# Two-layer encoder trunk on one core: all projections by seven products of quarters, output sums kept in DRAM, one buffer layout

## The chip, the core and the metric

The kernel runs on one core of a Trainium2 chip. Its engines work side by side: TensorE multiplies (PE in the profile, with PEld for its weight loads), VectorE (DVE) and ScalarE (ACT) work on elements, GpSimd (POOL) does a few small operations and issues some transfers, and SyncE (SP) issues the other transfers. The metric is the device time of one execution in microseconds; lower is better.

## The reference

The input is x of 512 tokens by 2048 features in float32. Two layers follow, each of the form x = layer_norm(ALPHA * x + mixer(x)).

```python
def attention_mixer(h, w_in, q_gain, k_gain, w_out, cos, sin):
    proj = h @ w_in
    q, k, v, g = jnp.split(proj, [A_WIDTH, A_WIDTH + A_KV_WIDTH, A_WIDTH + 2 * A_KV_WIDTH], axis=-1)
    ...
    q = apply_rope(rms_norm(q, q_gain), cos, sin) * (A_HEAD_DIM ** -0.5)
    k = apply_rope(rms_norm(k, k_gain), cos, sin)
    ...
        p = jax.nn.softmax(s, axis=-1).astype(v.dtype)
    ...
    return (o * jax.nn.silu(g)) @ w_out

def retention_mixer(h, w_in, decay_exp, w_out, cos, sin):
    proj = h @ w_in
    ...
    fwd = chunk_retention(q, k, v, log_g[0], strict=False)
    bwd = jnp.flip(chunk_retention(jnp.flip(q, 1), jnp.flip(k, 1), jnp.flip(v, 1), log_g[1], strict=True), 1)
    o = head_group_norm(fwd + bwd).reshape(B, S, R_V_WIDTH)
    return (o * jax.nn.silu(g)) @ w_out
```

Layer 1 is attention with 16 query heads of 128 and 4 key and value heads: w_in is 2048 x 5120, w_out 2048 x 2048. Layer 2 is retention with 8 heads (256 for q and k, 512 for v and the gate): w_in is 2048 x 12288, w_out 4096 x 2048. Nearly all the arithmetic is in these four projections.

## The kernel before, in words

**Arithmetic.** Every float32 operand is split into a high and a low part in a rounded format (`split`, L116 to L119: ScalarE casts the high part, VectorE subtracts it for the low part). A product is three matmuls, hi*hi, hi*lo and lo*hi (`mm3`, L261 to L265). A weight chunk is 128 x 1024 (512 KB): loaded by SyncE (`raw_load`), split by ScalarE and VectorE (L118 and L119, or L244 and L246 in layer 1 and the output projections), and used by TensorE in 12 or 24 matmuls. `next_chunk` keeps two chunks made ahead of the one in use (AHEAD = 2), and three pairs of chunk buffers (wp) hold them.

**Order of work.** TensorE's instructions stand in the order of the program text. Work that can wait is a generator (`Stream`), and `pump(us)` runs so many microseconds of it between the steps of a latency-bound part. So attention and retention steps are laced with projection matmuls.

**Layer 1** goes by four groups. For each: q by 512-wide matmuls (`n_form`), the rotary and norm work (`q_group`), attention (`att_group`: `scores`, four transposes and a split in `turn`, and `values`, which takes two heads together as 256 moving columns), laced with the gate projection (`t_form`, 512 wide), the next group's k and v (256 wide) and the last group's output projection (`out_proj`). The sums of the output projections stay in SBUF in y, added by VectorE (`accumulate`, L325 and L327).

**Between the layers** `out_proj_last` goes token block by token block, `norm_1` normalises, `turn_1` transposes into four quarters (token half by feature half), and the pools of layer 1 are closed before those of layer 2 open.

**Layer 2's input projection** is already done by quarters: the product of a 2x2 block matrix by seven block products instead of eight. `group(g)` goes through the seven products p; the activations' combinations are made once (`form`), the weights' combinations chunk by chunk on VectorE (`block_sum`, the adds at L212), with the names x, y and z for the three chains of PSUM banks (`CHAIN`). `evacuate` combines the banks, `deliver` rotates and transposes q and k and stores q, k, v and gates in DRAM (qkD, vD, gD).

**Retention** loads these per head, makes scores (`s_unit`, four per head), values (`o_unit`, four), norms and gates them (L880 to L884) and transposes (`o_close`). Each head's steps are laced with the output projection of the head before. At the change of pools after head 0, `residual` (L962 to L970) reads the normalised x back from DRAM and applies gain and bias. The last output projection goes token block by token block with `norm_2` and the stores of the result behind it.

## Time and profile before

| | |
|---|---|
| median of 3 timed runs | 2268.21 us (2267.46 to 2268.89) |
| the profiled execution's own time | 2264.06 us |
| its span | 2262.3 us |
| PE busy | 2188.5 us (97%) in 10448 matmuls |
| PEld / DVE / ACT / POOL busy | 81% / 70% / 42% / 9% |
| moved by DMA | 300.66 MB, mean 133 GB/s |

How to read it: matmuls are pipelined, so "busy" overlaps and the mean time of one matmul (390 ns) is not its price; the price is the distance between the starts of two in a row. A wait row reads "engine, what waited, <- what it waited for: us in total, times, longest". A group row reads "line, engine, operation, out<-in, shape xcount | busy us, mean ns | idle before". A window row reads "start:end length, busy us (count) for each engine, granted TensorE clock, share of the 16 DMA engines in use, GB/s".

### The profile page before, as it was taken

Reading aid. Unit: us, or ns where it says so; the run is one execution under the profiler, and the core shown is the slowest. Engines: PE = TensorE matmul, PEld = TensorE weight load, DVE = VectorE, ACT = ScalarE, POOL = GpSimd, SP = SyncE. Lnnn points to the kernel's source line nnn. Section 1 sums busy time; section 2 is a strip of 40 time slices with the busy share of each in tenths; the row PEclk is TensorE's granted clock in tenths of the full one; section 3 lists DMA queues with packets and bytes.
Section 4 is the critical chain, followed back from the end, with each engine's and each line's share of the span. In section 5 each row is a group of like instructions: output and inputs, shape, how many; then the busy total and the mean of one; then the engine's idle time right before and its main releaser. Section 6 shows DMA issues by size and latency. Waiting matters only on the chain.

```text
span 2262.3 us, 27514 instructions
## 1 busy us (share of the span) xinstructions
PE 2188.5 (97%) x10448; PEld 1830.5 (81%) x10448; DVE 1590.7 (70%) x2419; ACT 956.8 (42%) x1399; POOL 204.0 (9%) x247
## 2 busy tenths in 40 slices
PE   9999999999999979999999999999997699999997
PEld 8898888889888768888888888888886488888886
DVE  5565654655567897867787788778786766666667
ACT  4353243244245744444444444444464333333331
POOL 1201100200200000000000000000003400000004
PEclk9999999999999989999999999999999799999999
DMA  7312312322323364554465445545555433333332
GB/s 279 94 47 84 94 65 84 91 68 67 104 73 94 121 226 161 189 179 142 143 204 159 131 160 187 168 136 180 186 178 175 140 112 124 128 112 126 106 122 75
DMA packets 83557, 300.66 MB, mean 133 GB/s; under 512 B 10337, under 2 KB 11617, under 8 KB 81121
## 3 DMA queue, kind: packets, MB, share of 16 engines
q1 hardware_dynamic: 73440, 263.25, 36.0%
q0 software_dynamic: 9984, 35.66, 4.5%
q8 instruction: 82, 1.34, 0.2%
q14 instruction: 51, 0.41, 0.1%
HBM read 265.31 MB, written 33.55 MB: 132 GB/s over the span
## 4 chain that ended last, share of the span: by engine, by line
PE 91%; DVE 4%; POOL 2%; DMA 1%; issue 1%; ACT 1%; SPq 0%; POOLq 0%; DVEq 0%; ACTq 0%
PE acc L263 26%; PE acc L265 26%; PE acc L264 26%; PE tr L396 3%; PE o L263 2%; PE o L265 2%; PE o L264 2%; PE s L263 1%; PE s L264 1%; PE s L265 1%; POOL y L970 1%; DMA ln_bias<-in_ln_bias_dram 1%; DVE wlo L246 1%; DVE f L119 0%; DVE q_x L446 0%
## 5 line engine op out<-in xcount | busy, mean ns | idle before, releaser
L118 ACT CAST whi<-raw 128x1024 fp32r<-128x1024 f32 (+1 forms) x340 | 356.2, 1048 | 434.2 <-PE acc L265 393.2
L263 PE MATMUL acc<-whi,f 128*128 128x512 f32 x1344 | 526.1, 391 | 12.5 <-ACT whi L118 12.1
L264 PE MATMUL acc<-wlo,f 128*128 128x512 f32 x1344 | 523.9, 390 | 0.8 <-DVE wlo L119 0.7
L265 PE MATMUL acc<-whi,f 128*128 128x512 f32 x1344 | 523.7, 390 | 0.0
L119 DVE TENSOR_TENSOR wlo<-raw,whi 128x1024 fp32r<-128x1024 f32 (+1 forms) x340 | 409.5, 1212 | 154.0 <-ACT whi L118 149.8
L246 DVE TENSOR_TENSOR wlo<-raw,whi 128x512 fp32r<-128x512 f32 x324 | 215.2, 695 | 213.1 <-ACT whi L244 212.8
L244 ACT CAST whi<-raw 128x1024 fp32r<-128x1024 f32 x162 | 170.2, 1051 | 374.9 <-PE acc L265 192.2
L263 PEld LDWEIGHTS acc<-whi,f 128*128 128x128 f32 x1344 | 252.7, 188 | 65.1 <-ACT whi L118 12.5
L264 PEld LDWEIGHTS acc<-wlo,f 128*128 128x128 f32 x1344 | 252.8, 188 | 53.4 <-DVE wlo L119 1.9
L265 PEld LDWEIGHTS acc<-whi,f 128*128 128x128 f32 x1344 | 252.7, 188 | 52.6
L212 DVE TENSOR_TENSOR raw<-raw,raw 128x1024 f32<-128x1024 f32 x192 | 231.9, 1221 | 36.6 <-DMA raw<-in_wr_in_dram 35.5
L263 PE MATMUL acc<-whi,xT 128*128 128x256 f32 (+1 forms) x512 | 175.1, 342 | 4.9 <-ACT xT L118 4.9
L263 PE MATMUL acc<-whi,og 128*128 128x512 f32 x448 | 175.8, 392 | 0.0
L265 PE MATMUL acc<-whi,og 128*128 128x512 f32 x448 | 174.6, 390 | 0.0
L264 PE MATMUL acc<-wlo,og 128*128 128x512 f32 x448 | 174.6, 390 | 0.0
L265 PE MATMUL acc<-whi,xT 128*128 128x256 f32 (+1 forms) x512 | 173.6, 339 | 0.6 <-DVE xT L119 0.6
L264 PE MATMUL acc<-wlo,xT 128*128 128x256 f32 (+1 forms) x512 | 173.2, 338 | 0.0
L327 DVE TENSOR_TENSOR y<-acc,y 128x512 f32<-128x512 f32 x160 | 107.6, 686 | 26.7 <-PE acc L265 26.1
L263 PEld LDWEIGHTS acc<-whi,xT 128*128 128x128 f32 x512 | 98.3, 192 | 16.9 <-ACT xT L118 4.9
L265 PEld LDWEIGHTS acc<-whi,xT 128*128 128x128 f32 x512 | 98.2, 192 | 11.1 <-DVE xT L119 1.0
L264 PEld LDWEIGHTS acc<-wlo,xT 128*128 128x128 f32 x512 | 98.3, 192 | 10.1
L263 PE MATMUL acc<-xT,whi 128*128 128x512 f32 x256 | 102.6, 401 | 0.0
(184 smaller groups left out, 3355.8 us busy)
## 6 DMA issues: line engine op xcount, KB each, us to landing
raw<-in_wr_in_dram SPq DMA_DIRECT2D x248, 512.0 KB, 4.3
raw<-in_wr_o_dram SPq DMA_DIRECT2D x64, 512.0 KB, 3.6
raw<-in_wa_q_dram SPq DMA_DIRECT2D x32, 512.0 KB, 3.5
raw<-in_wa_g_dram SPq DMA_DIRECT2D x32, 512.0 KB, 3.5
raw<-in_wa_o_dram SPq DMA_DIRECT2D x32, 512.0 KB, 3.5
qkD<-qkT POOLq DMA_DIRECT2D x32, 256.0 KB, 5.4
vD<-t POOLq DMA_DIRECT2D x32, 256.0 KB, 5.0
raw<-qkD SPq DMA_DIRECT2D x16, 512.0 KB, 3.8
```

Source lines behind the costliest of these rows:

```text
L118: nc.scalar.copy(hi, src)
L119: nc.vector.tensor_sub(lo, src, hi.bitcast(F32))
L212: nc.vector.tensor_add(x, x, y)
L244: nc.scalar.copy(hi, raw[:, k])
L246: nc.vector.tensor_sub(lo[:, j], raw[:, k.start + j], hi[:, j].bitcast(F32))
L263: nc.tensor.matmul(ps, sh, mh, start=start, stop=False, skip_group_check=go_on)
L264: nc.tensor.matmul(ps, sh, ml, start=False, stop=False, skip_group_check=go_on)
L265: nc.tensor.matmul(ps, sl, mh, start=False, stop=stop, skip_group_check=go_on)
L327: nc.vector.tensor_add(yc, ps, yc)
L396: nc.tensor.transpose(out=b[:, tcols(i)], in_=src[:, tcols(i)], identity=ident)
L970: nc.gpsimd.tensor_add(y[:, t, cs], y[:, t, cs], gb[1])
```

## The change

All four projections now go by seven products of quarters, with one class `Block` for the weights, one class `Operand` for the activations and one generator `products`.

- Layer 1's input projection is five blocks of 1024 columns (k and v of all groups, then q and gate of each group), stored in DRAM (kD, vD, qD, gD); attention then runs as a second stage in two parts of two groups. The first is laced with the last input block, the second with the output projection of the first two groups.
- The output projections take two groups, or two heads, at a time: 1024 features in, two blocks of 1024 columns out, 14 chunks each. Their products are copied out of PSUM by ScalarE and added to a sum in DRAM (yD1, yD2) by GpSimd transfers that accumulate (`add_out`, `onto`). Only the last pair of each layer is added in SBUF (`Final`).
- The sums of weight quarters are in part made by accumulating transfers into the loaded chunk; a VectorE add is left in p = 6, and in p = 4 of the "lean" blocks (the third and later of each input projection).
- Attention values are made with tokens in the rows, one head at a time: 128 moving columns, and the division by the softmax sum is folded into the gate.
- The first two input blocks of each layer run as products (1, 2), (1, 2) and then (5, 6, 3, 7, 4) each.
- Retention runs two heads per pump stream; the residual of layer 2 is built during four input blocks, through DRAM.
- One layout: xp with 32 tiles of 128 x 1024, 9 raw chunks, 13 temporaries, 8 PSUM banks under one tag. No pool is closed.
- Rotary multiplications of layer 1 that GpSimd did are on VectorE. In `turn_1` gain and bias of the transposed x go half to ScalarE and half to VectorE.

```diff
-    ph = Pools(hp=24, tmp=6, rp=3, yp=1)
+    xp = ctx.enter_context(tc.tile_pool(name="xp", bufs=32))
+    rp = ctx.enter_context(tc.tile_pool(name="rp", bufs=9))
+    tmp = ctx.enter_context(tc.tile_pool(name="tmp", bufs=13))
...
+    def onto(x, src):
+        nc.gpsimd.dma_start(out=x, in_=src, accum_op=ALU.add)
...
+        def fetch(self, p, c):
+            if p == 1:
+                g["v" if self.lean else 1, c] = raw_load(q(11))
+            elif p == 2:
+                g[2, c] = raw_load(q(21))
+            elif p == 5 and not self.lean:
+                g["v", c] = raw_load(q(11))
+                onto(g["v", c], q(12))
+            elif p == 6:
+                g[3, c] = raw_load(q(22))
+            elif p == 7 and not self.lean:
+                g[7, c] = raw_load(q(12))
+                onto(g[7, c], q(22))
...
+        def make(self, p, c):
+            if p == 6:
+                nc.vector.tensor_add(v, v, g[3, c])
+            if p == 4 and self.lean:
+                nc.vector.tensor_add(v, v, g[2, c])
...
+        def follow(self, p, c):
+            if self.lean and p == 1:
+                onto(g["v", c], q(12))
+            elif self.lean and p == 3:
+                onto(g[3, c], q(12))
+            elif not self.lean and p == 6:
+                onto(g["v", c], q(21))
...
+    def add_out(yD):
+        def evacuate(blk, p):
+            nb, r, sign = ADDS[p]
+            for t in range(2):
+                o = temp("yo")
...
+                    nc.scalar.copy(o, blk.bk[CHAIN[p]][t])
...
+                onto(yD[:, r + t, blk.c0 + nb * 512:blk.c0 + nb * 512 + 512], o)
...
+        def products(self, b0, b1, op):
+            for seq in ((1, 5, 6, 3, 2), (7, 4)):
+                for b in (b0, b1):
+                    yield from products(b, op, seq, self.evacuate)
...
-                mm3(ob[:, :2 * P], (v[0][:, tcols(kb)], v[1][:, tcols(kb)]),
-                    [m[:, kb % 2] for m in pt[kb // 2]], kb == 0, kb == NT - 1)
+                mm3(self.ob[:, tcols(h)], [half(pT, i)[:, tcols(kb)] for i in range(2)],
+                    [half(self.v, i)[:, tcols(kb)] for i in range(2)], kb == 0, kb == NT - 1)
...
+    for i in range(R_HEADS // 2):
+        if i:
+            work = Stream(out_stream(r_out[i - 1], pairs[i - 1], out_pair(yD2)))
+        for h in (2 * i, 2 * i + 1):
+            heads[h].run(work, heads[h + 1] if h + 1 < R_HEADS else None, 4.5 if i else 2.5)
+        work.drain()
```

On TensorE, in retention, at the transposes that follow a value unit, before (tr is the transposes of a head's values o; acc is an output projection with the weights whi and wlo and the gated values og):

```order
L264 MATMUL acc_17261<-wlo_17175,og_16786 128x512
L265 MATMUL acc_17261<-whi_17174,og_16787 128x512
L396 MATMUL tr_17378<-ident,o_17303 128x128 x4
L263 MATMUL acc_17262<-whi_17174,og_16786 128x512
L264 MATMUL acc_17262<-wlo_17175,og_16786 128x512
L265 MATMUL acc_17262<-whi_17174,og_16787 128x512
```

In the second head of each pair there stands now (o is a value unit, made of the values inh and inl and the scores pTh and pTl):

```order
L203 MATMUL o_16632<-inl_16385,pTh_16463 128x512
L204 MATMUL o_16632<-inh_16384,pTl_16464 128x512
L407 MATMUL tr_16661<-ident,o_16619 128x128 x4
L202 MATMUL o_16667<-inh_16378,pTh_16461 128x512
L203 MATMUL o_16667<-inl_16379,pTh_16461 128x512
L204 MATMUL o_16667<-inh_16378,pTl_16462 128x512
```

The projection matmuls that stood around a transpose are gone from there: the stream of a pair is used up two scores into its second head, and the transposes of one unit follow the matmuls of the next directly.

On TensorE, in attention, a turn of one head's probabilities and the values that follow it, before (vh and vl are the parts of the values, pTh and pTl those of the transposed probabilities; the last number is the count of moving columns):

```order
L265 MATMUL acc_1078<-xT_92,wlo_917 128x512
L396 MATMUL tr_1096<-ident,p_1006 128x128 x4
L263 MATMUL o_1105<-pTh_1013,vh_393 128x256
L264 MATMUL o_1105<-pTl_1014,vh_393 128x256
L265 MATMUL o_1105<-pTh_1013,vl_394 128x256
```

And now:

```order
L204 MATMUL acc_2690<-whi_2963,f_581 128x512
L407 MATMUL tr_3124<-ident,p_3032 128x128 x4
L202 MATMUL o_3045<-v_2884,pT_3037 128x128
L203 MATMUL o_3045<-v_2884,pT_3037 128x128
L204 MATMUL o_3045<-v_2884,pT_3037 128x128
```

Twelve matmuls of 256 columns for two heads became twelve of 128 columns for each head: 384 matmuls in all before, 768 now.

On GpSimd, in the output projections of retention, before (only the reciprocal roots of the heads' norms stand there):

```order
L379 TENSOR_TENSOR rstd_16258<-rs_e_16259,neg_half 128x1
L379 TENSOR_TENSOR rstd_16320<-rs_e_16321,neg_half 128x1
L379 TENSOR_TENSOR rstd_16365<-rs_e_16366,neg_half 128x1
L379 TENSOR_TENSOR rstd_16713<-rs_e_16714,neg_half 128x1
L379 TENSOR_TENSOR rstd_16751<-rs_e_16752,neg_half 128x1
```

And now (raw is a weight chunk that a transfer adds to, yD the sum in DRAM, yo a product copied out of PSUM):

```order
L114 DMA yD_6300<-yo_14880 128x512
L114 DMA raw_15021<-in_wr_o_dram 128x1024
L114 DMA raw_15040<-in_wr_o_dram 128x1024
L390 TENSOR_TENSOR rstd_14911<-rs_e_14912,neg_half 128x1
L114 DMA yD_6300<-yo_14943 128x512
L114 DMA yD_6300<-yo_14946 128x512
L114 DMA raw_15186<-in_wr_o_dram 128x1024
L114 DMA raw_15237<-in_wr_o_dram 128x1024
L390 TENSOR_TENSOR rstd_15002<-rs_e_15003,neg_half 128x1
```

The roots now stand in one queue with the accumulating transfers of weights and of output sums.

More of the change, by code (lines that the diff above doesn't have):

```diff
@@ new lines, in encoder_trunk_kernel, with fetch_to, make_chunk @@
+    ready = []
+    fetched, taken = [0], [0]
+    def fetch_to(n):
+        while fetched[0] < min(len(order), n):
+            blk, p, c = order[fetched[0]]
+            blk.fetch(p, c)
+            fetched[0] += 1
+    def make_chunk():
+        blk, p, c = order[len(ready)]
+        raw = blk.make(p, c)
+        hi, lo = [wp.tile([P, CH], F32R, tag=n, name=nm(n)) for n in ("whi", "wlo")]
+        split(hi, lo, raw)
+        blk.follow(p, c)
+        ready.append([(half(hi, j), half(lo, j)) for j in range(2)])
@@ L911, in run @@
                 nxt.load_v()
[L913 to L914 removed]
+            work.pump(2 * each)
             self.o_close(NT - 1)
[L916 to L917 removed]
     lnp = []
@@ L1009, in _rope_angles @@
+    fin = Final(yD2)
+    fin.load()
+    work = Stream(out_stream(r_out[-1], pairs[-1], fin.products))
+    work.pump(20.0)
+    ln_params()
+    work.until(lambda: 0 in fin.rows)
+    norm_2(0)
+    norm_2(1)
+    work.drain()
+    norm_2(2)
+    norm_2(3)
 def _rope_angles(np, hd):
```

1196 lines of the change are left out of this document (552 added, 644 removed).

## The prediction

> **What bounds the kernel now.** I read the page first: busy shares and the chain that ended last.
>
> ```profile
> PE 2188.5 (97%) x10448; PEld 1830.5 (81%) x10448; DVE 1590.7 (70%) x2419; ACT 956.8 (42%) x1399; POOL 204.0 (9%) x247
> PE 91%; DVE 4%; POOL 2%; DMA 1%; issue 1%; ACT 1%; SPq 0%; POOLq 0%; DVEq 0%; ACTq 0%
> ```
>
> TensorE is nearly always at work and 91% of the chain is matmuls, so the time is the matmul stream plus TensorE's waits. Then the waits, TensorE's alone:
>
> ```profile
> PE s L263 <- DVE f L871: 27.6, 1, 27.6
> PE acc L263 <- ACT whi L118: 12.1, 1, 12.1
> PE o L265 <- DVE pT L119: 6.4, 1, 6.4
> PE acc L263 <- DVE t L757: 0.4, 1, 0.4
> ```
>
> Two single waits, 27.6 and 12.1 us, are most of what it loses before the end. The timeline gives the price of one matmul as the distance of starts: 512 columns, 256 columns, and transposes of 128.
>
> ```profile
> 899.79 0.39 PE L265 MATMUL acc<-whi,f 128*128 128x512 f32 x1
> ...
> 901.83 0.39 PE L265 MATMUL acc<-whi,f 128*128 128x512 f32 x1
> 19.82 0.28 PE L264 MATMUL acc<-wlo,xT 128*128 128x256 f32 x1
> ...
> 23.91 0.28 PE L265 MATMUL acc<-whi,xT 128*128 128x256 f32 x1
> 752.72 0.60 PE L396 MATMUL tr<-ident,y 128*128 128x128 f32 x4
> 753.07 0.48 PE L263 MATMUL acc<-whi,ogh 128*128 128x512 f32 x1
> 753.38 0.40 PE L264 MATMUL acc<-wlo,ogh 128*128 128x512 f32 x1
> ```
>
> The first pair is nine steps apart: 2.04 / 9 = 0.2267 us. The second is 34 steps: 4.09 / 34 = 0.120 us. Four transposes take 0.35 us, 0.0875 each, and the next matmul starts 0.31 instead of 0.23 us later, so a group of four costs 0.43 us.
>
> **Term 1, the matmul stream.** Counted from the two programs' orders. Matmuls of 512 columns: 8640 before, 8496 after; 144 x 0.2267 = 32.6 us less. That is small because q, k, v, gates and both output projections lose an eighth, but k and v come over from the 256-wide ones. Those, 768 for k and v and 384 for attention values, all go: 1152 x 0.120 = 138.2 us less. New are 768 matmuls of 128 columns. No row shows one; the transposes have that width and also load new weights each, so I take 0.0875: 67.2 us more. Bounds: 0.060 (half of the 256-wide) gives 46, and 0.2267 (no cheaper than 512) gives 174. Sixteen more groups of transposes: 6.9 us. Sum: -32.6 - 138.2 + 67.2 + 6.9 = **-96.7 us**.
>
> **Term 2, waits that go.**
>
> ```profile
> DVE y L969 <- DMA ln_gain<-in_ln_gain_dram: 20.9, 3, 12.2
> 790.00:800.00 10.00, 2.16 (x8) 1.36 (x8) 10.00 (x14) 5.08 (x7) 1.46 (x2) 0.50 0.64 216
> ```
>
> The 27.6 us wait is the change of pools after head 0: the next score's multiply (L871) stands on VectorE behind the residual's (L969), which wait for the gain from DRAM. The 12.1 us wait is the first weight chunk behind the forms that could only start when layer 1's pools were closed: VectorE is busy for all of these 10 us. The residual now stands inside four input blocks, and nothing is closed: **-39.7 us**. What is late next stands in term 3.
>
> **Term 3, waits that come.**
>
> (a) Second heads. A pair's stream is 28 chunks x 12 x 0.2267 = 76 us, and the pump calls ask for 15 x 4.5 = 67.5 us per head, so it ends early in the second head, and that head's chain lies open. Its links:
>
> ```profile
> L880 DVE BATCH_NORM_STATS2 o_st<-o 128x6 f32<-128x512 f32 x32 | 22.2, 695 | 17.3 <-PE o L265 17.3
> L379 POOL TENSOR_TENSOR rstd<-rs_e,neg_half 128x1 f32<-128x1 f32 x40 | 25.9, 649 | 588.7 <-DVE rs_e L378 576.3 <-ACT whi L244 12.3
> L390 DVE TENSOR_SCALAR nmr<-mv,rstd 128x1 f32<-128x1 f32 x36 | 7.7, 213 | 19.6 <-POOL rstd L379 19.0
> L883 ACT ACTIVATE o<-o,nmr,rstd 128x512 f32<-128x512 f32 x32 | 24.9, 779 | 67.9 <-DVE nmr L390 67.8
> L884 DVE TENSOR_TENSOR o<-o,g 128x512 f32<-128x512 f32 x32 | 22.1, 690 | 12.8 <-ACT o L883 12.8
> ```
>
> These are 3.03 us; with two small steps and handoffs I estimate 4.0 from a value unit's end to its transposes. The next unit covers 12 x 0.2267 = 2.72 us. So the waits are 4.0 - 2.72 = 1.3 us, none, 0.9, and 2.7 for the last, with 0.6 for the last score's split ahead and 1.5 for the first form of the next projection: 7 us, four times: **+28 us** (0 if GpSimd and VectorE answer at once, 50 if each step queues).
>
> (b) Attention's two ends, where turns and values stand without filler: I take 5 us each, near the 6.4 us wait of the first retention head above: **+10** (4 to 20).
>
> (c) The layer's border: two row blocks are normalised after the products (1, 5, 6, 3, 2) of both blocks, with 4 us of matmuls as cover; statistics and norm need some 7 us by the rows in (a), then eight turns press on ScalarE: **+8** (0 to 15).
>
> (d) p = 7 and 4 share a bank chain and follow one another in four input blocks (0.4 us each by the wait above) and in `Final`, where an add and its statistics for each of two tiles, steps of 0.69 us, stand before: some 1.1 us, four times. **+6** (2 to 10).
>
> (e) The end. After the last matmul there were 14 us with one row block to normalise; now there are two:
>
> ```profile
> 2248.00:2262.30 14.30, 0.52 (x3) 0.10 (x1) 10.34 (x15) 0.81 (x1) 6.95 (x6) 0.70 0.35 129
> L941 DVE SCALAR_TENSOR_TENSOR y<-y,rstd,ln_bias 128x512 f32<-128x512 f32 x9 | 8.9, 988 | 0.1
> ```
>
> VectorE was busy 10.3 of 14.3 us there; four more such steps of 0.99: **+4** (2 to 8).
>
> (f) VectorE in layer 1. Its two first blocks are 56 chunks (152 us of matmuls). VectorE has to do 56 low parts, 8 adds and 22 steps of forms, 86 x 1.22, 12 combinations of 0.68, and 8 rotations of about 3.9 (six steps of 0.42, two of 0.68):
>
> ```profile
> L469 DVE TENSOR_TENSOR r_dst<-q_x,tabs 128x256 f32<-128x256 f32 x32 | 12.7, 413 | 0.0
> L753 DVE TENSOR_TENSOR t<-acc,t 128x512 f32<-128x512 f32 x24 | 15.4, 683 | 0.0
> L119 DVE TENSOR_TENSOR wlo<-raw,whi 128x1024 fp32r<-128x1024 f32 x336 | 407.8, 1221 | 151.2 <-ACT whi L118 147.0 <-DMA raw<-in_wr_in_dram 3.5
> 800.00:1640.00 840.00, 833.72 (x3724) 690.59 (x3725) 666.13 (x725) 385.63 (x424) 50.84 (x84) 0.99 0.52 169
> ```
>
> That is 105 + 8 + 31 = 144 us, 95% of the matmuls' time; at 79% (the window) TensorE lost 6 us in 840. Three pairs of chunk buffers cover 8 us of backlog. **+8** (0 to 30).
>
> (g) Transfers. 336 now accumulate: 224 weight chunks of 524 KB and 112 sums of 262 KB. Their issue costs GpSimd little, if it is that of a plain one:
>
> ```profile
> L729 POOL DMA_DIRECT2D vD<-t x32 | 17.4, 545 | 398.4 <-DVE t L753 330.4 <-DVE t L757 66.1 <-issue 1.2
> ```
>
> 336 x 0.55 = 185 us on an engine that was busy for 204 of 2262. But an accumulate reads its target too. No row shows one. Lower bound: a plain load; upper: a load and a store of the same bytes, twice. I take twice. In the middle of retention, one pair's stream of 28 chunks carries 10.5 MB plain, 6.3 MB x 2 of weights, 7.3 MB x 2 of sums, and a head's 3.1 MB: 41 MB, within 76 us plus the first head's 18. That is 436 GB/s. The most that the trace shows over 5 us is
>
> ```profile
> 10.00:15.00 5.00, 4.42 (x31) 4.07 (x30) 4.00 (x7) 3.91 (x6) 0.00 (x0) 1.00 1.03 419
> q1 hardware_dynamic: 73440, 263.25, 36.0%
> ```
>
> so 41 MB take 41 / 0.415 = 99 us where 94 are there: 5 us over, three times: **+15** (0 at the lower bound). The first two blocks of each layer in (5, 6, 3, 7, 4) need 42 MB in 113 us, 372 GB/s, and fit.
>
> The Trainium skill ("Collectives: The Full Stack", section "The bandwidth ceiling") says that an add inside a DMA needs two source reads on the same ring, so that a reduce runs at about half the rate of a copy. That is a rule against this change; no run here shows it. By it (g) stays at 15 and the forecast stands; without it (g) is 0 and the forecast 15 us lower.
>
> Sum of term 3: 28 + 10 + 8 + 6 + 4 + 8 + 15 = +79 us. Altogether -96.7 - 39.7 + 79 = -57.4 us: a span of 2204.9 us. The profiled execution took 2264.06 us for its span of 2262.3, and the median shown is 2268.21, 4.15 above; 2204.9 + 1.8 + 4.15 = **2211 us**.
>
> Priced at nothing: the way of q, k, v and gates of layer 1 through DRAM (stored blocks earlier than loaded; only group 3's come from the block just done, with the attention of groups 0 to 2, over 100 us, as cover, and a store and a load of some 5 us each if it were gone); the residuals through DRAM, 12 us of VectorE in four blocks of 76 us; the divisions folded into the gate, which only takes steps from VectorE. The start is as before, since half the tokens and a half chunk are enough for the first matmuls.
>
> **Rivals.**
>
> R1, slower: transfers bound the stages with accumulates. Mechanism: GpSimd's queue serves weights, sums and roots in one order, and the engines move less than in the best 5 us. The whole run's rate per share is 263.25 MB / (0.36 x 2262.3 us) = 323 GB/s. At that, 41 MB take 127 us, 33 over, three times; and 42 MB take 130 us, 17 over, twice: 133 us instead of 15, so **2329 us**. It decides below 356 GB/s: there the excess is 3 x 21 + 2 x 5 = 73 us, and the gain is gone. For: twice the bytes is what the operation must move, and only nine raw chunks buffer it. Against: 419 GB/s was reached with plain 512 KB loads, and lean blocks have four chunks of time (10.9 us) for an add.
>
> R2, slower: a 128-column matmul costs as much as 512 columns: 768 x (0.2267 - 0.0875) = 107 us more, **2318 us**; it eats the gain from 0.162 us on. For: nothing in the trace is that narrow except transposes. Against: from 512 to 256 the price fell in proportion.
>
> R3, faster: VectorE and transfers keep up and narrow matmuls cost 0.060: -8 - 15 - 21 and half of (b) and (c) gone: 2211 - 53 = **2158 us**.
>
> That the change does less than it says is excluded by the counts of matmuls.
>
> **How the numbers follow.** The forecast, 2175 to 2250: 0.48. R3, below 2175: 0.08. R1, 2250 to 2330: 0.30; a fifth of it still faster than before, an eighth within 0.2%. R2: 0.09. Some queue that I do not see, slower than before: 0.05. A change under 0.2% (4.5 us) cannot be told from none. Faster: 0.48 + 0.08 + 0.06 = 0.62; same: 0.04; slower: 0.34. The range runs from 2165, just inside R3, to 2310, with most of R1: left out are R2's 0.09, the top of R1, and the bottom of R3, 2 in 10 together. The forecast's own range is 2175 to 2250.
>
> **What would show it.** PE's sum: about 97 us less in starts. Starts 0.0875 us apart in the 128-wide values; 0.2267 would be R2. In PE's waits no 27.6 and 12.1 us, but rows of 1 to 3 us before transposes of o in the second heads. DMA share: near 1.0 with weights waiting ("ACT whi <- DMA raw", or "PE acc <- DVE wlo" behind it) in the output stages would be R1; a share under 0.8 there would make (g) wrong. VectorE above 95% in the first 300 us, with PE waiting for wlo, would make (f) larger. A PE idle sum over 150 us makes the forecast wrong whatever its cause.

## The result and the profile after

The changed kernel takes 2365.72 us (median of four runs, 2361.47 to 2369.4) against 2268.55 (2267.46 to 2271.44): 1.0426 times as long, interval 1.0403 to 1.0448. It is slower by 97 us, where 57 less were forecast. The profiled execution has a span of 2361.3 us against 2262.3.

The page, busy shares and chain, to be set beside the two lines of before:

```profile
PE 2181.9 (92%) x9984; PEld 1787.1 (76%) x9984; DVE 1639.1 (69%) x2183; ACT 1192.3 (50%) x1568; POOL 533.1 (23%) x583
PE 62%; DMA 13%; DVE 12%; issue 7%; ACT 3%; POOL 3%; SPq 0%; POOLq 0%; ACTq 0%; DVEq 0%
```

TensorE has 464 instructions less and is busy for almost as long as before, and the chain, 91% matmuls before, is 62% matmuls now. Its waits, where two single ones of 27.6 and 12.1 us were most of the loss:

```profile
PE acc L203 <- DVE wlo L103: 30.6, 26, 5.9
PE acc L202 <- DVE y L368: 24.9, 4, 16.7
PE tr L407 <- DVE o L870: 22.8, 10, 4.3
PE acc L202 <- ACT whi L102: 19.2, 7, 8.9
PE acc L202 <- ACT f L102: 14.9, 6, 4.6
PE tr L407 <- ACT p L615: 12.1, 3, 6.3
PE tr L407 <- DVE rs_e L389: 6.7, 2, 3.6
```

Both old waits are gone. In their place stand 84 short waits, 58 of them in these rows, the longest but one of 8.9 us, for many different things: weight chunks (wlo, whi), the last projections' sums (y), the second heads (o, rs_e), first forms (f), attention's exponentials (p).

**Work and loss.** To compare the two I price each matmul by the distance of starts and call the rest loss. The price that was missing, 128 columns (the attention's values):

```profile
406.84 0.28 PE L203 MATMUL o<-v,pT 128*128 128x128 f32 x1
...
407.96 0.27 PE L204 MATMUL o<-v,pT 128*128 128x128 f32 x1
```

These are ten steps: 1.12 / 10 = 0.112 us. So the work after is 8496 x 0.2267 + 768 x 0.1117 + 180 groups of transposes x 0.43 = 2089 us, and before it was 8640 x 0.2267 + 1152 x 0.120 + 164 x 0.43 = 2167. From the first matmul to the last, before takes 2243.3 us and after 2336.7: the loss is 76 us before and 248 after. The work fell by 78 us and the loss rose by 172; with 6 us more behind the last matmul that is the 99 us between the spans.

The loss by stage, with the windows of the page's engines for the same stages (the columns: length; busy us and instructions of PE, PEld, DVE, ACT, POOL; granted clock; DMA share; GB/s):

```profile
0.00:160.00 160.00, 122.69 (x477) 94.00 (x478) 102.20 (x138) 76.17 (x89) 57.10 (x41) 0.93 0.86 264
160.00:392.00 232.00, 229.11 (x1025) 187.63 (x1023) 168.84 (x227) 119.52 (x144) 83.39 (x63) 1.00 0.70 182
392.00:734.00 342.00, 316.79 (x1876) 273.74 (x1875) 226.55 (x409) 194.43 (x339) 56.20 (x61) 0.94 0.58 141
734.00:853.00 119.00, 106.30 (x463) 85.62 (x463) 101.29 (x148) 63.56 (x89) 15.09 (x21) 0.91 0.73 210
853.00:1738.00 885.00, 876.95 (x3910) 720.41 (x3908) 623.81 (x723) 423.05 (x480) 152.11 (x205) 1.00 0.70 185
1780.00:2240.00 460.00, 405.80 (x1716) 325.05 (x1715) 288.10 (x384) 252.03 (x356) 128.70 (x156) 0.93 0.88 224
2240.00:2361.30 121.30, 82.30 (x340) 65.85 (x338) 96.36 (x113) 38.92 (x40) 33.14 (x27) 0.84 0.49 139
```

| stage | forecast waits | loss after |
|---|---|---|
| layer 1's inputs, 0 to 392 us | 8 (f) | 54.7 |
| attention, to 734 | 10 (b) | 45.6 |
| first last projection and layer border, to 853 | 8 (c) | 21.7 |
| layer 2's inputs, to 1738 | none of its own | 14.9 |
| retention heads, to 2240 | 43 (a, g) | 85.7 |
| last projection, to the last matmul | none of its own | 25.2 |

(d), 6 us, was spread over four of them. The right column is the whole loss, so what was lost there before and stays (36 us in all) is in it. The forecast was a loss of 76 - 39.7 + 75 = 111 us; it is 248.

**Half clock.** The granted clock is 0.84 to 0.94 in the five windows where a large part is lost, and 1.00 in the two where only about 2% is (160 to 392 us, and 853 to 1738). After a second head's wait of 3.48 us:

```profile
1967.65 0.76 PE L407 MATMUL tr<-ident,o 128*128 128x128 f32 x4 [3.48 <-DVE o L870]
1968.06 0.78 PE L202 MATMUL s<-inh,inh 128*128 128x512 f32 x1
1968.63 0.63 PE L203 MATMUL s<-inl,inh 128*128 128x512 f32 x1
1969.06 0.63 PE L204 MATMUL s<-inh,inl 128*128 128x512 f32 x1
```

and that window in the list of windows:

```profile
1967.60:1971.00 3.40, 3.32 (x10) 2.22 (x10) 2.37 (x2) 0.59 (x1) 0.00 (x0) 0.57 0.66 202
```

Starts are 0.43 us apart instead of 0.2267. Summed over all matmuls that started late without a wait in front while the granted clock was 0.5, this is some 54 us (6 before): part of the 248, and in no term of the forecast.

**Transfers.** The two kinds of queue, with packets, MB and share of 16 engines' span (before: 4.5 and 36.0%):

```profile
q0 software_dynamic: 62848, 195.07, 40.4%
q1 hardware_dynamic: 80880, 252.77, 31.6%
```

**GpSimd.** Its reciprocal roots of q, 128x4 elements each, and two of them in order of time:

```profile
L390 POOL TENSOR_TENSOR q_rs<-rs_e,neg_half 128x4 f32<-128x4 f32 x16 | 75.3, 4704 | 51.9 <-DVE rs_e L389 51.9
```

```profile
70.28 10.82 POOL L390 TENSOR_TENSOR q_rs<-rs_e,neg_half 128x4 f32<-128x4 f32 x1 [6.66 <-DVE rs_e L389]
81.07 1.79 POOL L114 DMA_DIRECT2D raw<-in_wa_in_dram  x2
...
82.83 13.44 POOL L390 TENSOR_TENSOR q_rs<-rs_e,neg_half 128x4 f32<-128x4 f32 x1
...
96.87 3.62 POOL L114 DMA_DIRECT2D raw<-in_wa_in_dram  x4
```

The longest takes 13.4 us and the shortest 1.04. Four weight sums stand behind it, and the chain of waits goes on from there:

```profile
98.00 16.99 DMA raw<-in_wa_in_dram
...
115.09 1.04 ACT whi L102
```

That is TensorE's wait of 8.9 us at 116 us.

### The profile page after: what moved, and what is told of

Same layout as the page of the kernel before. It is cut to its first block, busy times and chain, and to the rows that moved or that the text cites. A ratio compares the mean times of both kernels' runs of the same rounds, so it can differ in the third digit from the quotient of the medians.

```text
span 2361.3 us, 27594 instructions
## 1 busy us (share of the span) xinstructions
PE 2181.9 (92%) x9984; PEld 1787.1 (76%) x9984; DVE 1639.1 (69%) x2183; ACT 1192.3 (50%) x1568; POOL 533.1 (23%) x583
## 3 DMA queue, kind: packets, MB, share of 16 engines
q0 software_dynamic: 62848, 195.07, 40.4%
## 4 chain that ended last, share of the span: by engine, by line
PE 62%; DMA 13%; DVE 12%; issue 7%; ACT 3%; POOL 3%; SPq 0%; POOLq 0%; ACTq 0%; DVEq 0%
PE acc L204 17%; PE acc L203 17%; PE acc L202 17%; DVE wlo L103 5%; DMA raw<-in_wr_in_dram 4%; DMA raw<-in_wa_in_dram 3%; DMA raw<-in_wr_o_dram 3%; PE tr L407 3%; PE o L203 2%; PE o L204 2%; ACT whi L102 2%; PE o L202 1%; PE s L204 1%; DVE f L103 1%; PE s L202 1%
## 5 line engine op out<-in xcount | busy, mean ns | idle before, releaser
L103 DVE TENSOR_TENSOR wlo<-raw,whi 128x1024 fp32r<-128x1024 f32 (+1 forms) x645 | 786.4, 1223 | 439.0 <-ACT whi L102 434.5
L202 PE MATMUL acc<-whi,f 128*128 128x512 f32 x2576 | 1032.1, 401 | 60.9 <-DVE y L368 24.9
L203 PE MATMUL acc<-wlo,f 128*128 128x512 f32 x2576 | 1022.7, 397 | 31.2 <-DVE wlo L103 30.6
L102 ACT CAST whi<-raw 128x1024 fp32r<-128x1024 f32 (+1 forms) x645 | 676.3, 1051 | 732.6 <-PE acc L204 562.9
L204 PE MATMUL acc<-whi,f 128*128 128x512 f32 x2576 | 1019.6, 396 | 3.2 <-DVE f L103 3.1
L202 PEld LDWEIGHTS acc<-whi,f 128*128 128x128 f32 x2576 | 493.4, 192 | 169.5 <-issue 27.4
L203 PEld LDWEIGHTS acc<-wlo,f 128*128 128x128 f32 x2576 | 493.8, 192 | 142.4 <-DVE wlo L103 43.7
L204 PEld LDWEIGHTS acc<-whi,f 128*128 128x128 f32 x2576 | 492.8, 191 | 111.6 <-DVE f L103 7.6
L114 POOL DMA_DIRECT2D raw<-in_wr_in_dram x104 | 91.5, 879 | 392.4 <-DVE wlo L103 201.2
L114 POOL DMA_DIRECT2D yD<-yo x112 | 102.3, 1052 | 246.2 <-ACT yo L338 170.3
L103 DVE TENSOR_TENSOR f<-xf,f 128x1024 fp32r<-128x1024 f32 (+2 forms) x77 | 86.0, 1125 | 8.1 <-ACT f L102 7.7
L102 ACT CAST f<-xf 128x1024 fp32r<-128x1024 f32 (+2 forms) x77 | 73.8, 969 | 23.9 <-DVE xf L249 12.9
L202 PE MATMUL o<-v,pT 128*128 128x128 f32 x256 | 74.0, 289 | 0.0
L204 PE MATMUL o<-v,pT 128*128 128x128 f32 x256 | 72.2, 282 | 0.6 <-DVE pT L103 0.6
L869 ACT ACTIVATE o<-o,nmr,rstd 128x512 f32<-128x512 f32 x32 | 24.9, 778 | 94.7 <-DVE nmr L401 94.7
L203 PE MATMUL o<-v,pT 128*128 128x128 f32 x256 | 72.2, 282 | 0.0
```

The costliest lines, as they stand in the source:

```text
L102: nc.scalar.copy(hi, src)
L103: nc.vector.tensor_sub(lo, src, hi.bitcast(F32))
L114: nc.gpsimd.dma_start(out=x, in_=src, accum_op=ALU.add)
L202: nc.tensor.matmul(ps, sh, mh, start=start, stop=False, skip_group_check=go_on)
L203: nc.tensor.matmul(ps, sh, ml, start=False, stop=False, skip_group_check=go_on)
L204: nc.tensor.matmul(ps, sl, mh, start=False, stop=stop, skip_group_check=go_on)
```

## The experiments

Theories: **A**, the accumulating transfers take twice as long, and weight chunks come late; **B**, short chains of small steps lie open and cost their wait and the half clock behind it; **C**, GpSimd's queue, where small steps stand with the accumulates; **D**, engines that work in order stand at a load issued just ahead; **E**, the smaller buffer for software transfers (the change had halved it, which the prediction passed over). All kernels have the same 9984 matmuls and so the same work; what differs is loss. The losses by stage, each from one profiled execution (the runs of one kernel spread by up to some 10 us, so a difference of a few us between two rows alone shows nothing):

| kernel | us | ratio to before | inputs 1 | attention | border | inputs 2 | heads | last | all |
|---|---|---|---|---|---|---|---|---|---|
| changed | 2365.7 | 1.0426 | 54.7 | 45.6 | 21.7 | 14.9 | 85.7 | 25.2 | 248 |
| all plain | 2296.3 | 1.0129 | 36.8 | 36.2 | 19.3 | 4.0 | 62.4 | 21.5 | 180 |
| weights plain | 2307.8 | 1.0175 | 38.7 | 37.7 | 19.4 | 4.3 | 73.8 | 20.6 | 194 |
| roots on VectorE | 2325.5 | 1.0261 | 46.8 | 46.4 | 21.5 | 13.6 | 60.6 | 21.7 | 211 |
| thinner filler | 2321.7 | 1.0245 | 55.1 | 45.8 | 21.7 | 16.4 | 38.1 | 30.0 | 207 |
| last mixed | 2360.3 | 1.0410 | 51.8 | 46.1 | 21.8 | 16.0 | 87.4 | 23.8 | 247 |
| loads ahead | 2357.4 | 1.0402 | 59.4 | 29.3 | 20.8 | 14.6 | 89.5 | 25.0 | 239 |
| larger ring | 2372.8 | 1.0464 | 52.0 | 53.2 | 22.7 | 15.4 | 85.1 | 25.8 | 254 |
| mended | 2293.2 | 1.0113 | 61.8 | 29.4 | 23.1 | 13.5 | 27.4 | 19.1 | 174 |
| mended, plain | 2237.1 | 0.9871 | 40.0 | 22.3 | 17.3 | 5.0 | 23.7 | 13.1 | 121 |
| mended, roots | 2284.7 | 1.0076 | 53.1 | 29.4 | 23.4 | 13.5 | 29.2 | 21.3 | 170 |
| with VectorE's adds | 2270.9 | 1.0021 | 38.0 | 28.3 | 24.7 | 18.0 | 28.3 | 21.3 | 159 |
| forms early | 2245.3 | 0.9900 | 39.8 | 25.1 | 22.9 | 16.1 | 6.6 | 22.5 | 133 |

### All accumulates as plain transfers

```diff
+    def plain(x, src):
+        nc.gpsimd.dma_start(out=x, in_=src)
...
-                onto(g["v", c], q(12))
+                plain(g["v", c], q(12))
...
-                onto(yD[:, r + t, blk.c0 + nb * 512:blk.c0 + nb * 512 + 512], o)
+                nc.gpsimd.dma_start(out=yD[:, r + t, blk.c0 + nb * 512:blk.c0 + nb * 512 + 512], in_=o)
```

(and the four other weight sums)

> All 336 accumulating transfers (224 sums of weight quarters, 112 sums of output projections) become plain transfers of the same tiles on the same queue: the additions are left out, everything else stays. In the profile of after an accumulating packet of 4 KB took 328 ns where a plain one took 159, and 762 us of 16 engines' time went into them. Theory A (transfers): the doubled transfers fill the DMA engines at the start and in the retention pairs and arrive late; then TensorE's waits behind weight chunks (38 us for wlo and 21 us for whi) go almost wholly, with the half-clock time behind them: 2365 - 70 = 2295 us, between 2275 and 2310. Theory B (short chains of small steps that lie open in the second heads, in attention and at both final projections, each followed by matmuls at half clock): transfers matter for 20 us, 2345. Theory C (GpSimd: its small power steps take 1 to 13 us where VectorE is full, and accumulates stand behind them in its queue): plain transfers stand in the same queue, so half of the start's loss stays: about 2325.

2296.33 us, ratio 1.0129 (1.0114 to 1.0144): 69 us less, as A had it. The software queue in this kernel's page:

```profile
q0 software_dynamic: 55680, 195.07, 24.9%
```

The same 195.07 MB take 0.249 x 2294.1 = 571 us of 16 engines, with accumulates 0.404 x 2361.3 = 954. The gain lies where A said, 17.9 us in layer 1's inputs and 23.3 in the heads, and also where it had not, 10.9 in layer 2's inputs and 9.4 in attention. But 180 us of loss stay without one accumulate. No other single edit below gives as much; the transfers are the largest single cause found, and not the only one.

### Weight sums alone as plain transfers

```diff
-                onto(g["v", c], q(12))
+                plain(g["v", c], q(12))
```

(and the four other weight sums)

> Only the 224 weight sums become plain transfers (the addition of the second quarter is left out); the 112 sums of the output projections still accumulate. By the packets' time the weights hold 588 of 762 us. A: the gain of all plain transfers, 69 us, divides like that: 2365 - 53 = 2312 us, with the loss in the start and in the input blocks of layer 2 as in the kernel without any accumulate, and half of the gain in the retention pairs. If the order of GpSimd's queue counts rather than the volume (C), the sums that wait for their evacuated tiles still hold up what stands behind: 2330.

2307.84 us, ratio 1.0175 (1.0156 to 1.0194): 58 of the 69 us, in every stage before the heads as without any accumulate, in the heads 11.9 of 23.3. A's division by packet time, 53 us, holds to 5 us.

### The roots off GpSimd

```diff
-        nc.gpsimd.tensor_tensor(out=dst, in0=e[:, :n], in1=neg_half[:, :n], op=ALU.pow)
+        nc.vector.reciprocal(dst, e[:, :n])
```

> Every small power step of GpSimd becomes a reciprocal on VectorE, right behind the step that feeds it: the square root is left out, all instructions else stay. C: the start loses the two power steps of 10.8 and 13.4 us that held four accumulates and attention the waits for p (12.8 us) with their half clock: 2365 - 45 = 2320 us, and the wait of 8.9 us at 116 us is gone. A: the transfers stay as they are, so at most 10 us: 2355. B: the chains of the second heads get some 0.4 us shorter per link: -8, 2357.

2325.45 us, ratio 1.0261 (1.0246 to 1.0277): C's total, but not C's places. The start gives 8 us and the heads 25. In the heads small roots stood behind accumulates that waited for their own first load, as here in the changed kernel's chain of waits:

```profile
1941.33 9.78 DMA raw<-in_wr_o_dram
...
1951.76 0.87 POOL raw L114
1952.62 0.59 POOL rstd L390
...
1955.06 1.10 PE tr L407 x4
```

With the roots elsewhere, TensorE's waits before the transposes of o (for o and rs_e) fall from 29.5 to 21.8 us in the heads, and three waits for weight low parts (13.6 us) are gone too. That those came because the weights' accumulates stood behind roots is argued from the order of the queue. The run also shortens the chains, B's 8 us, and doesn't tell that apart. In attention nothing changes, and its wait is still in this kernel's list:

```profile
PE tr L407 <- ACT p L615: 11.8, 3, 6.1
```

C's reading of attention fell.

### A thinner filler

```diff
-            heads[h].run(work, heads[h + 1] if h + 1 < R_HEADS else None, 4.5 if i else 2.5)
+            heads[h].run(work, heads[h + 1] if h + 1 < R_HEADS else None, 2.5)
```

> In the three retention pairs that run beside an output projection each pump call asks for 2.5 us of matmuls instead of 4.5, so that the projection lasts through the second head as well. B: the 33.6 us of waits in the second heads of these pairs (o, rs_e, f, pTl) and some 12 us of half clock behind them go: 2365 - 40 = 2325 us. A: the same transfers now spread over both heads, the waits for weight chunks there (14 us with 5 of half clock) go too: together down to 2305; if the transfers were the limit of the whole stage (DMA share 0.94 over 391 us), nothing is gained because the stage stays that long: 2360. C: GpSimd's queue is no lighter, at most -10.

2321.71 us, ratio 1.0245 (1.023 to 1.0261). The heads' loss falls from 85.7 to 38.1: B's waits before the transposes of o from 29.5 to 8.5 us, the half clock behind waits from 22 to 8, and the 13.6 us for weight low parts are gone as well. The heads in the windows of this kernel:

```profile
1782.00:2194.00 412.00, 388.06 (x1715) 315.88 (x1714) 282.19 (x383) 247.94 (x354) 132.30 (x153) 0.97 0.95 237
```

48 us shorter at a DMA share of 0.95 for 0.88, so the transfers were not the limit of the stage. With the projection spread over both heads the accumulates have more time as well: TensorE's wait for low parts in the whole run falls from 30.6 to 16.7 us. Plain transfers (23 us), roots off the queue (25) and thinner filler (48) take the same waits from three sides and don't add up: once the filler is thinner, plain transfers give the heads only 3.7 us (27.4 to 23.7, the mended kernels of the table).

### The last projection mixed

```diff
     work.until(lambda: 0 in fin.rows)
+    work.pump(5.6)
     norm_2(0)
+    work.pump(5.5)
     norm_2(1)
     work.drain()
```

> In the last projection the normalisation of the first two row blocks is no longer put ahead of all remaining evacuations on VectorE: 5.6 us of matmuls are issued first, then row block 0, then 5.5 us more, then row block 1. B: the wait of 16.7 us and the 4.4 us of half clock shrink to about 5: 2365 - 12 = 2353 us, with the tail behind the last matmul some 3 us longer. A and C: the wait is for sums loaded from DRAM or for GpSimd, so nothing changes: 2365.

2360.32 us, ratio 1.041 (1.0392 to 1.0427): the interval holds the changed kernel's 1.0426, so no gain is shown. The waits for y fell from 24.9 to 17.1 us (the longest from 16.7 to 7.3), but the half clock in that stage rose from some 4 to 8 us.

### Loads ahead of their use

```diff
                 if h == 1:
-                    t2 = t + 2
-                    if t2 < NT:
-                        g.load_q(t2)
...
+                    step(t + 2, "fetch_kv", "fetch_q")
+                if h == 3:
+                    step(t + 2, "load_kv", "load_q")
```

(and for the residual, `soon(4, finish)` behind the load, in `a_in[3]` for `a_in[2]`)

> In the attention the loads of the next group's k and v and of the next q are issued two units (some 8 us) before they are split into high and low parts, and the first ones eight matmul groups ahead of the stage; the residual's loads are issued three chunks (8 us) before ScalarE multiplies them and stand one input block later. Nothing else changes. Theory D (an engine that works in order stands still until a load issued just before has landed, and the weight chunk or the exponential behind it is late): attention's loss of 46 us falls to 20, the start's by 10 to 15: 2365 - 38 = 2327 us. Theory A (transfers as such): the loads are late because the DMA engines are full, and land late ahead of time too: -10, 2355. Theory C (GpSimd's power steps): no change in attention.

2357.36 us, ratio 1.0402 (1.0384 to 1.0421): 8 of the 38 us, and the interval overlaps that of the changed kernel. D is right in attention, where the loss falls from 45.6 to 29.3, not to 20; every later kernel with these loads has 22 to 29 there. How it arose, in the changed kernel's chain of waits:

```profile
426.91 5.43 DMA kv<-vD
432.37 0.63 ACT v L102
433.01 0.70 DVE v L103
433.74 0.88 ACT p L615 x2
434.66 0.66 PE tr L407 x4
```

ScalarE stood at the split of the next group's v until it landed, with the exponential of a tile long scored behind it. At the start the loss doesn't move (49.4 us in the first 160, both times), but D was not tested there, because the residual's transfers did not move either. The rows tell min, median and max duration in ns, then the first and last start in us, in the changed kernel and in this one:

```profile
L531 SPq DMA_DIRECT2D xr<-in_x_dram x8: 328/409/733, 96.9 to 152.9; - x8
L531 SPq DMA_DIRECT2D xr<-in_x_dram x8: 328/433/1026, 96.9 to 151.9; - x8
```

The program text ties these loads to the third input block before and to the fourth now; on the chip they are issued in the first two blocks both times.

### A larger buffer for software transfers

```diff
-dynamic_dma_scratch_size=2048
+dynamic_dma_scratch_size=4096
-    tmp = ctx.enter_context(tc.tile_pool(name="tmp", bufs=13))
+    tmp = ctx.enter_context(tc.tile_pool(name="tmp", bufs=12))
```

> The changed kernel with the buffer for software transfers put back from 2048 to 4096 bytes, which the change had halved beside its other edits; one temporary tile less (12 for 13) makes room. Theory E (the small buffer holds up GpSimd's queue): the accumulates go out earlier, 2365 - 30 = 2335 us. All others: no change, 2365, or a few us more for the missing tile.

2372.83 us, ratio 1.0464 (1.0451 to 1.0478): E falls: no stage with accumulates gains more than 3 us. The 7 us more lie in attention (53.2 for 45.6), with one temporary tile less.

### The mended order, with and without accumulates

```diff
-            heads[h].run(work, heads[h + 1] if h + 1 < R_HEADS else None, 4.5 if i else 2.5)
+            heads[h].run(work, heads[h + 1] if h + 1 < R_HEADS else None, 2.3 if i else 1.5)
...
     norm_1(0)
+    work.pump(5.6)
     norm_1(1)
-    work.pump(4.0)
...
+    work.pump(11.2)
     norm_2(0)
+    work.pump(5.5)
     norm_2(1)
     work.drain()
```

(with the loads ahead of the kernel above)

> The accumulating transfers all stay. Loads ahead as in the run beside it; the filler in the retention pairs 2.3 us per call (1.5 in the first pair) so that some matmuls are left for the border to the next pair; the normalisations of the finished row blocks put between the last evacuations at both final projections. B and D (open chains, late loads): 2365 - 38 - 54 - 8 (last projection) - 8 (layer border) = 2257 us, 10 less than before. A: the doubled transfers bind the stages, 2300 at best.

> The same with all 336 accumulates as plain transfers (their additions left out). It tells what the accumulates cost once the order is mended. A: as much as before the mending, 60 to 70 us less than the run beside it, some 2190. B and D: the mended order has room for them, 10 to 25 us less, and 2235.

2293.18 us (1.0113, 1.0098 to 1.0128) and 2237.09 (0.9871, 0.9853 to 0.989). Order alone gives 72 of the 97 us back, not the 108 of B and D; and the accumulates still cost 56 us in the mended order, 22 of them in layer 1's inputs, where the mending had brought nothing (54.7 before it, 61.8 with it). A was nearly right on their price, 56 to 69 us where it had 60 to 70; B and D, with 10 to 25, were not. That 2237 is so near the 2235 of B and D is chance: their two errors cancel.

### Roots by group, and adds on VectorE

```diff
-                    rsqrt(q_rs[:, g, t], ss, 1.0 / P, RMS_EPS)
+                    nc.vector.tensor_scalar(q_rs[:, g, 4 * t:4 * t + 4], ss, 1.0 / P, RMS_EPS, op0=ALU.mult, op1=ALU.add)
...
         def load_kv(self):
+            nc.gpsimd.tensor_tensor(out=q_rs[:, self.g], in0=q_rs[:, self.g], in1=neg_half, op=ALU.pow)
```

> The mended kernel with one change: the roots of layer 1's q are no longer taken by GpSimd block by block (16 steps on 128x4) but group by group just before the attention (4 steps on 128x16); the accumulates stay. C: the two steps of 10.8 and 13.4 us at 70 and 83 us no longer hold the accumulates in GpSimd's queue, and the start's wait of 8.3 us for a weight chunk goes with its half clock: 2293 - 12 = 2281 us. A: the accumulates come late because they take long, so -3: 2290.

```diff
+            if self.dve and p in (5, 7):
+                g["t", c] = x4("qt", F32)
+                nc.sync.dma_start(out=g["t", c], in_=q(12))
...
+            if self.dve and p in (5, 7):
+                m = v if p == 5 else g[3, c]
+                nc.vector.tensor_add(m, m, g["t", c])
```

> As the run beside it, and in eleven of the input blocks (two of layer 1, nine of layer 2) the sums of weight quarters are made as a plain load into a tile of its own and an add on VectorE, 8 steps of 1.22 us per block of 76 us, instead of 88 accumulates. A: these blocks' loss (13 us in the rest of layer 1's input, 13.5 in layer 2's) falls to some 5 together: 20 us below the run beside it, 2261, level with the kernel before. Rival: VectorE becomes the bound there (69% busy in the plain stretch, 79% then) or the plain loads of all quarters on one queue come as late: no gain, 2281.

The roots: 2284.73 us (1.0076, 1.0061 to 1.0091), 8.5 us less, some 7 of it in the first 160 us, where C had the long roots.

The adds: 2270.88 us (1.0021, 1.001 to 1.0032), 14 less, but not by the adds. The loss in layer 1's inputs falls from 53.1 to 38.0, all of it in the matmuls that the changed kernel runs in its first 160 us (41.4 to 24.4). They are over by 136 us here, and the first add runs at 188. What changed at the start is the residual: its loads, at 97 to 145 us in the kernel with the roots by group, now start at 229 us. The rows of the adds and of the residual's loads in this kernel, and the window from 100 to 150 us without the adds and with them:

```profile
L156 DVE TENSOR_TENSOR raw<-raw,qt x88: 1214/1225/1226, 188.1 to 1637.4; 128x1024 f32<-128x1024 f32 x88
L539 SPq DMA_DIRECT2D xr<-in_x_dram x8: 327/328/328, 228.9 to 306.7; - x8
```

```profile
100.00:150.00 50.00, 38.07 (x132) 28.53 (x131) 20.68 (x34) 19.33 (x22) 13.83 (x18) 0.86 1.03 325
100.00:150.00 50.00, 44.91 (x193) 35.06 (x192) 33.09 (x54) 21.90 (x25) 15.96 (x17) 1.00 0.96 253
```

So the 17 us at the start are argued to be the price of the residual among the accumulates; no run moved it alone. Where the adds run, nothing was gained: the rest of layer 1's inputs lost 13.6 us for 11.7, layer 2's 18.0 for 13.5. A's 20 us are not shown, and which half of the rival holds is open: VectorE is 80% busy in layer 2's inputs for 71%, and the waits for loads there did not grow.

### Forms early

```diff
-        op.form(1)
         for at, n in (((1, 0), 5), ((5, 0), 6), ((5, 1), 2), ((6, 0), 3), ((6, 1), 4), ((3, 0), 7)):
...
+        pairs[i].form(1)
         work.drain()
```

(also at both attentions, whose filler is 1.4 and 1.95; the turns of the layer's border by columns; adds on VectorE in layer 1's two blocks alone)

> As the kernel with VectorE's adds, but with the adds only in the two blocks of layer 1 (the accumulates are back in layer 2), and three more open chains closed: the first form of each output projection's operand is made before the last matmuls of the stream ahead are drained, not after; the filler of both attentions is a little thinner (1.4 and 1.95 us for 1.7 and 2.3) and the second q of a stage is split one unit later; the turns of the first two row blocks at the layer's border go by quarter of the columns, so that the next layer's first product can start after four of eight. B and D: the borders of the pairs lose 14 us of waits with 7 of half clock, attention 8, the layer's border 8, and the adds in layer 2 that came late give back 4: 2271 - 40 = 2231 us, 1.6% less than before. Rival (each stage is held by its transfers, and a wait that is closed comes back as a wait for a weight chunk): 2260 to 2271. By this run the accumulates, which are 292 of 336 still, do not decide whether the change loses, but the order of the small steps around them does; if it stays at 2265 or more they do.

2245.27 us, ratio 0.99 (0.9885 to 0.9915): 1.0% less than the kernel before, 14 us short of the forecast but below all that the rival allowed. 320 of the 336 accumulates are still there (the expectation's 292 is a miscount). By the test that the expectation sets, the accumulates do not decide whether the change loses; the order of the small steps around them does, and the residual's late place (230 to 308 us here too) is part of that order. The page and the heads' window of this kernel:

```profile
PE 2141.3 (95%) x9984; PEld 1760.1 (78%) x9984; DVE 1645.2 (73%) x2199; ACT 1194.0 (53%) x1572; POOL 479.1 (21%) x555
```

```profile
1735.00:2121.00 386.00, 382.67 (x1739) 314.92 (x1738) 284.30 (x389) 252.18 (x358) 128.01 (x154) 1.00 0.99 254
```

The heads run at full clock with a loss of 6.6 us, and the DMA share is 0.99: the transfers just fit into the matmuls' time. The heads gave 21.7 us where 21 were expected; attention and border gave 5, not 16.

## Why the prediction was wrong

The sign was wrong. Term 1's work and term 2's two waits came as forecast but for one price; term 3 failed: 75 us of waits ahead of the last matmul were forecast on top of the 36 that stay, and the loss is 248. Each of its waits was priced alone, as a bare chain or an excess of volume; the half clock, the late loads and the residual were priced at nothing. The amounts below overlap and can't be added up.

- **Term 1**, -96.7: -78. The counts are right. The 128-column matmul costs 0.112 us, not 0.0875: 768 x 0.024 = 18.6 us. The transposes were the wrong nearest row. R2 (0.2267) is wrong.
- **Term 2**, -39.7: both waits are gone.
- **(a), second heads**: right place and mechanism, too small. Links were priced at their bare durations and the wait alone; with roots held up in GpSimd's queue (VectorE waited 59.7 us for them in all, 19.0 before) and half clock after most waits, the heads lose 85.7 us where (a) and (g) gave 43. The thinner filler took 48 us away with nothing else changed.
- **(b), attention**, 10: 45.6. "Priced at nothing: the way of q, k, v and gates of layer 1 through DRAM" was a step that failed. The data were stored long before; the load and the split that needs it were issued together. Taking them apart gave 16 us; what holds the remaining 29 was not settled.
- **(c), (d), the border**: about 8 us of waits for y (L368), where some 2 were priced; a loss of 21.7 in the stage, which none of the reorderings lowered.
- **(d), (e), the end**: the 16.7 us wait is of the kind that was not seen, whole normalisations put ahead of evacuations on VectorE, and these take twice as long while GpSimd multiplies beside them (first the step nearly alone, then GpSimd's product and the step beside it, then the late evacuation):

```profile
2308.90 0.75 DVE L924 SCALAR_TENSOR_TENSOR y<-y,mv,ln_gain 128x512 f32<-128x512 f32 x1
...
2309.25 1.52 POOL L938 TENSOR_TENSOR y<-y,ln_gain 128x512 f32<-128x512 f32 x1 [1.18 <-ACT y L937]
...
2309.62 1.70 DVE L924 SCALAR_TENSOR_TENSOR y<-y,mv,ln_gain 128x512 f32<-128x512 f32 x1
...
2321.87 1.27 DVE L368 TENSOR_TENSOR y<-y,acc 128x512 f32<-128x512 f32 x2
```

  With that order mixed the longest such wait was 7.3 us, but the time did not fall clear of noise. The tail behind the last matmul is 20 us for 14, where +4 was forecast.
- **(f), layer 1's VectorE**, 8 with a bound of 30: 54.7 in that stage. Some 18 us of it are accumulates and about 8 roots on GpSimd; 37 remain without accumulates. VectorE's own load was not measured apart, but one stretch of the changed kernel tells its size:

```profile
50.00:100.00 50.00, 39.11 (x165) 29.01 (x164) 46.27 (x55) 26.75 (x31) 34.89 (x17) 1.00 0.61 139
```

  VectorE is busy for 46 of these 50 us, and TensorE lost 14 us, mostly waiting for VectorE's rotations and low parts; 12 with plain transfers, 14 with the roots elsewhere. By that VectorE's own load cost some 12 us, near (f)'s 8. The rest is what it had not: "the residuals through DRAM" stood among the things priced at nothing. Layer 1's residual, 8 loads and 8 stores of 512 KB, runs at 97 to 160 us, on top of the 42 MB that (g) put into 113 us there: 50 MB would be 446 GB/s, above the 419 that (g) had as the most. By the kernel with VectorE's adds it cost some 17 us (argued, as said there).
- **(g), transfers**, 15: 69, or 56 in the mended order. (Its 15 takes 0.415 MB per us where the row has 419 GB/s; by that it is 12.) The unit price was right, an accumulate takes about twice a plain transfer's time (1.9 times, worked out at the end), as the Trainium skill ("Collectives: The Full Stack", section "The bandwidth ceiling") has it for a reduce against a copy: the trace agrees. What failed is that the excess of volume over time in one stage was taken for the whole cost. The start and layer 2's inputs, which "fit", lost 29 us to late chunks at shares of 0.86 and 0.70, since an accumulate must wait for its first load, then takes its turn in GpSimd's queue. R1's mechanism was half right, its stages right, its sum of 118 us too large.
- **Half clock**: no term at all, and some 54 us. It makes a wait of 3.5 us cost five or six.

R1 gave 2329 us and R2 2318; neither reaches 2366, since no one mechanism does. The forecast's own last test, "A PE idle sum over 150 us makes the forecast wrong whatever its cause", is what happened: the list of TensorE's waits sums to 154 us, some 175 by the distances of starts. What stays open: 25 to 29 us in attention, some 20 at the layer's border, and how the start's loss divides between VectorE, the residual and the accumulates.

## What to carry to other kernels

Saving 78 us of matmuls on a kernel with few waits pays only as long as the waits of the new order stay below that: here many small ones cost their length and then some us of matmuls at half clock, and 84 of them ate the gain twice; the last kernel, with the order mended, kept 1.0%. Price a transfer that adds not only by its bytes but by its place: a load, then a queue, then twice the time; and look at what else is in that queue. When something is sent through DRAM, issue the load well ahead of the instruction that uses it, and keep filler matmuls until the last open chain is closed. Look in the trace when a transfer really starts: the residual's place in the program text was not its place in time, and an edit that only moved it in the text did nothing.

## What the runs showed of the hardware

- A matmul of 128 columns takes 0.112 us from start to start and one of 512 takes 0.2267: 0.87 against 0.44 ns a column; 256 columns took 0.120. Below 256 columns hardly anything is saved.
- Of 26 waits of TensorE of 2 us and more in the changed kernel (the start's apart), 24 were followed within 4 us by at least 1 us at a granted clock of 0.5; in 5 of them it stood at 0.5 already. Of 38 waits of 0.3 to 1 us, 10 were, and 8 of these stand beside a wait of over 1.3 us. The Trainium skill ("TensorE: Matmul & The Clock Gate", section "HAM oscillation — how this bites in real kernels") sets the limit at gaps of more than about 3.4 us; here the clock fell after shorter ones too, of 2.04, 2.58 and 2.85 us.
- GpSimd's root on 128x4 elements took 1.04 to 13.4 us; the two longest (10.8 and 13.4) ran while VectorE worked, with hardly a pause, mostly through steps on two tiles of 1024 columns. During the second of them VectorE shows:

```profile
85.06 1.22 DVE L103 TENSOR_TENSOR wlo<-raw,whi 128x1024 fp32r<-128x1024 f32 x1
86.20 1.22 DVE L152 TENSOR_TENSOR raw<-raw,raw 128x1024 f32<-128x1024 f32 x1
```

  The Trainium skill ("SBUF — State Buffer", section "Who interferes with whom") says that a VectorE instruction with two inputs in SBUF contends with a GpSimd instruction that reads SBUF; the trace agrees, and in both directions: 1.70 us for VectorE's 0.75 beside GpSimd's products.
- Accumulating transfers used 383 us more of 16 engines' time than plain ones of the same 147 MB (954 against 571 us for the queue, whose other 48 MB are plain in both). By bytes the plain ones took 147 / 195 of the 571, 430 us, so an accumulate took 1.9 times a plain transfer.
